# A new issue order, and a new split of copies and scalings between two engines, in a two-layer decoder trunk

## The chip, the cores and the metric

The kernel runs on one core of a Trainium2 chip. The core has a matrix engine (TensorE, PE), a vector engine (VectorE, DVE), a scalar engine (ScalarE, ACT), GpSimd (POOL) and SyncE (SP), each with its own instruction stream that it works off in order; transfers between device memory and the on-chip buffers are started by SP and ACT. The metric is the device time of one execution in microseconds (us), less is better.

## What is computed

The reference is a trunk of two layers over 256 tokens of width 1024, float32, conditioned by a vector `c`. Layer 0 has two groups of attention heads (a sliding window with sinks, and sparse attention with a compressed, a selected and a window branch); layer 1 has block attention, which for 256 tokens is causal attention with 16 heads.

```python
def reference(x, c, w_ada, b_ada, norm_g, w_in_even, ..., w_in_odd, w_out_odd, final_g):
    cos, sin = rope_tables(x.shape[1])
    c_act = jax.nn.silu(c)
    for layer in range(DEPTH):
        ada = jnp.einsum('bd,de->be', c_act, w_ada[layer]) + b_ada[layer]
        shift, scale, gate = jnp.split(ada, 3, axis=-1)
        h = rms_norm(x, norm_g[layer]) * (1.0 + scale[:, None, :]) + shift[:, None, :]
        if layer % 2 == 0:
            y = even_mixer(h, ...)      # oa*silu(za), ob*silu(zb), joined, @ w_out_even
        else:
            y = odd_mixer(h, ...)       # moba_attention(q, k, v) * silu(z), @ w_out_odd
        x = x + gate[:, None, :] * y
    return rms_norm(x, final_g)
```

## The kernel before

**Numbers.** Every large product is computed in three passes of a reduced format (`mm3`): a float32 operand is split into `hi` (a copy by ACT into `whi`, `hhi` or `ghi`) and `lo` (the difference, by DVE, into `wlo`, `hlo` or `glo`), and PE sums hi·hi, hi·lo and lo·hi in one bank. So each weight that is loaded (into one of five buffers `raw`, named raw_106 to raw_110 in the order listings) passes through ACT and DVE before PE can use it.

**Stages.** At the start, layer 0's shift and scale are made group by group (`START`, `start_ada`, `start_sums`) from parts of `w_ada`, which are loaded into whatever room is free: `qT`, `oT`, `gate`, `kTb`, `t`. Meanwhile rows of `w_in_even` come into `raw` (`start_row`: 1304 columns and 384 columns, two transfers each), and `start_mm` sums their products with the normalised input, 24 matmuls for each row block and 8 row blocks. `xs` holds the 256 tokens of `x`. Then come layer 0's two attention groups, its output projection, and beside them the sums over `w_ada` that layer 1 needs (DVE multiplies `raw` by `cz` and adds: the gate's sum into `acc`, the shift's and scale's into raw_110, whose last parts are loaded into raw_109). Then layer 0's result is added to `xs` (`t<-ps_pj,gate`, `xs<-xs,t`), the norm of layer 1 follows (`ISA` on `xs` is the sum of squares), then layer 1's projections, attention and output projection, and the last norm: for the last 256 columns of the last 128 tokens `xs<-ps_pj_101,xs`, the sum of squares, the root (ACT), the reciprocal (DVE), the multiplication by `final_g` (it lies in `bigA`), the scaling in three pieces, three transfers out.

**The order.** The body of the kernel issues nothing: class `Plan` records every operation with what it depends on (`record`), and `issue` (line 279) then emits all of them in the order of a table of 2985 numbers, `ORDER` (line 35), each engine getting its part of that one order. A second table, `FLIP` (line 164), holds numbers of operations that go to the other one of ACT and DVE than the code names: `copy`, `scaled` and `affine` ask for it in `either` (line 234). An engine waits at its next instruction until what it depends on is done, and nothing behind it passes. All instructions carry the line in `record` that makes the deferred call, L276 (in the changed kernel L275), so they are told apart by the names of their tiles.

```python
    def either(self, eng):
        other = self.vector if eng is self.scalar else self.scalar
        return other if len(self.ops) in FLIP else eng
```

Of the kernel before, what the change touches and what calls it, by code (L numbers as in the profile page):

```python
# [35 lines left out]
49 7 6 4 0 1 9 21 22 23 2 3 47 5 91 41 42 48 92 89 24 25 26 27 28 29 30 93 73 88 50 31 90 32 74 99 58 33 75 34  # L36
98 35 51 77 59 94 52 76 36 46 44 45 60 54 37 53 10 11 38 61 12 13 14 63 95 78 79 15 97 16 132 17 126 96 64 128
101 127 18 19 20 62 129 100 102 103 104 105 106 107 108 109 110 111 112 113 114 115 116 117 130 133 55 83 158
118 65 56 66 68 80 67 119 159 84 85 121 86 120 81 131 69 122 174 175 176 177 178 179 180 181 168 82 70 143 160
140 170 134 123 137 87 171 39 161 40 124 149 138 169 172 155 150 146 144 71 162 135 173 72 147 141 125 163 182  # L40
183 184 185 186 187 188 189 190 191 192 193 152 194 142 195 153 201 165 196 136 197 151 199 198 164 154 156 202
148 203 157 139 200 238 207 226 204 205 239 240 166 214 227 208 228 206 220 209 167 232 215 235 212 236 241 268
221 280 242 243 269 218 223 281 233 210 145 229 230 278 216 213 237 222 244 211 250 270 234 282 259 262 271 251
283 224 252 279 225 247 219 265 284 256 272 231 245 257 285 263 273 286 287 288 289 290 291 292 293 217 294 295
296 297 264 298 258 299 307 274 246 300 248 301 249 275 303 302 260 266 253 308 254 309 255 267 261 324 304 336
311 305 310 337 333 277 345 318 325 306 346 339 313 276 338 312 342 319 314 343 372 326 316 344 315 348 373 380
322 8 381 320 378 379 375 374 377 376 472 530 334 327 328 382 335 360 366 361 383 362 329 349 340 341 350 347
369 330 384 331 332 354 385 363 351 357 317 386 387 388 389 390 391 392 393 394 395 396 397 321 355 398 356 323
399 367 405 400 368 401 364 402 358 359 406 365 370 407 371 352 403 442 409 443 408 430 436 411 473 418 410 353
433 424 527 420 445 404 431 434 412 446 413 425 421 533 427 428 416 432 439 422 474 414 423 475 1003 939 476 691  # L50
477 417 415 435 444 466 429 451 440 441 447 437 463 478 480 482 484 479 481 483 485 486 487 438 488 460 419 489
495 454 455 491 490 469 470 493 464 492 426 496 448 499 457 467 494 497 471 529 456 500 509 501 449 498 510 511
524 450 502 503 617 525 452 458 618 465 619 620 531 453 468 461 550 506 462 942 459 556 512 551 513 813 514 526
507 554 504 557 508 552 505 521 555 522 534 518 536 553 515 537 516 541 538 519 606 542 520 938 539 517 535 607
528 544 543 608 937 547 540 676 564 565 566 567 568 569 576 694 577 612 578 579 609 580 581 588 589 590 613 558
523 610 611 591 592 593 549 600 601 602 559 639 545 692 603 604 621 614 622 623 624 560 695 561 625 548 562 563
570 571 615 572 605 573 626 627 640 631 628 629 632 641 574 575 630 582 693 583 633 634 635 814 935 636 643 644
645 646 584 642 638 585 940 586 587 647 594 595 670 596 597 669 546 598 637 599 668 648 649 816 650 651 663 653
661 662 696 697 698 699 700 671 654 701 652 702 664 703 818 943 689 819 936 655 817 656 43 657 665 658 704 666
705 706 667 707 708 815 709 660 710 711 659 672 673 712 713 674 714 715 716 944 717 941 746 747 748 749 945 532  # L60
683 675 946 947 948 949 754 950 951 952 953 750 752 954 955 956 957 756 753 958 959 960 961 677 684 1029 751 678
774 775 776 777 962 1032 682 757 758 780 679 680 963 685 681 718 820 782 781 964 778 719 821 686 759 784 687 720
755 822 721 722 786 688 723 965 823 971 824 779 724 966 972 785 868 869 870 871 760 967 787 968 872 761 878 969
783 768 973 974 975 976 977 978 979 980 876 981 982 983 984 763 874 985 986 987 988 769 762 788 880 1150 879 789
970 896 897 898 899 1030 1218 989 877 764 765 881 904 990 796 825 906 725 991 873 902 726 826 791 727 728 992
729 900 730 875 731 993 732 827 616 908 766 797 994 882 998 995 1000 1001 999 1031 767 1087 1088 1089 1090 996
790 905 770 1002 771 1648 1221 997 1033 772 828 1091 829 1004 830 690 831 1005 832 883 733 1093 1006 773 734
1097 1007 901 833 1095 834 792 1092 1008 793 794 891 1113 1114 1115 1116 1151 885 795 1009 1010 1011 1012 903
1034 798 799 1013 800 835 735 909 736 836 884 837 838 801 839 1152 1037 737 738 890 739 740 907 1014 886 887
1015 888 1121 1096 840 1350 741 1016 742 1094 841 1349 1123 842 1038 843 1017 1039 889 1040 844 1117 845 1035  # L70
743 910 846 1119 847 848 849 911 1219 892 850 1122 1041 1042 1043 851 1118 1153 1154 1155 1156 919 1018 1036 744
893 852 1098 853 894 1044 1045 1019 1046 913 1339 1047 854 1220 855 912 856 1048 1049 895 1050 1051 1052 1020
1053 1054 857 1157 1222 858 1419 859 1159 914 915 916 1418 1163 802 803 804 805 806 807 808 809 1160 1021 1161
917 1022 1099 1223 918 1124 1179 1180 1181 1182 1120 1100 1023 745 1164 920 921 922 1055 1056 1102 1024 1057
1189 1058 1059 1107 1060 1025 1226 1227 923 1228 1125 1183 1061 1062 1126 1108 860 810 1063 1064 1229 1230 1026
1101 1027 1187 1162 861 1340 862 863 1127 1065 1231 864 1133 1232 1233 1234 1028 865 1235 1185 1224 1236 1237
1103 1341 1104 1105 924 925 926 927 928 929 930 931 1106 1158 1225 1426 1128 811 1276 1277 1278 1279 866 1351
1423 1109 1134 1422 1110 1111 1066 1165 1188 1238 1282 1239 1240 1241 1067 1112 1284 1068 1166 1286 1069 1174
1070 1242 1352 1243 1129 1130 1184 1131 1244 1285 1071 1245 1072 1073 1167 1074 1280 1075 1427 1246 1247 1248
1249 1250 1251 1252 1253 1254 1132 1420 1186 1190 1076 1077 812 1255 1173 1135 1136 1137 1168 1191 1421 1302  # L80
1303 1304 1305 1138 1436 1342 1343 1344 1345 1312 1428 1169 1287 1306 1170 1171 1429 1192 1256 867 1078 1172
1079 1257 1258 1080 1199 1308 1259 1260 1313 1261 1262 1263 1264 1265 1281 1266 1267 1268 1283 1269 1081 1082
1310 1437 1083 1194 1175 932 1176 1177 1084 1450 1311 1270 1346 1451 1178 1288 1452 1424 1646 1193 1271 1272
1273 1085 1453 1195 1196 1274 1197 1289 1086 1353 1354 1355 1356 1198 1200 1425 1359 1139 1140 1141 1142 1143
1144 1145 1146 1147 1148 1307 933 1309 1275 1432 1440 1433 1201 1361 1202 1203 1357 1454 1430 1204 1444 1445
1290 1446 1291 1447 1448 1363 1442 1449 1292 1149 1293 1294 1431 1205 1206 1207 1208 1209 1210 1211 1212 1213
1214 1379 1380 1381 1382 1438 1297 1314 934 1508 1296 1295 1315 1439 1317 1316 1298 1362 1299 1215 1300 1493
1455 1364 1441 1456 1492 1457 1216 1462 1347 1463 1301 1458 1385 1464 1358 1459 1217 1318 1322 1465 1319 1360
1434 1320 1460 1461 1323 1468 1469 1365 1321 1387 1470 1366 1443 1466 1367 1324 1325 1368 1326 1471 1467 1327
1474 1435 1374 1496 1472 1369 1370 1526 1497 1371 1328 1329 1330 1331 1332 1333 1334 1335 1336 1337 1389 1509  # L90
1372 1383 1527 1373 1390 1384 1375 1494 1376 1377 1386 1534 1535 1388 1558 1536 1378 1391 1475 1392 1537 1495
1393 1538 1559 1394 1560 1528 1473 1395 1400 1396 1510 1397 1399 1561 1338 1562 1511 1398 1476 1529 1348 1563
1401 1402 1403 1477 1404 1478 1498 1479 1405 1406 1407 1408 1409 1410 1411 1412 1413 1414 1499 1530 1415 1539
1649 1540 1531 1416 1650 1588 1417 1512 1513 1541 1542 1564 1565 1480 1481 1543 1486 1487 1482 1488 1483 1489
1484 1490 1485 1491 1544 1500 1532 1545 1778 1566 1546 1504 1547 1548 1533 1549 1567 1550 1655 1568 1551 1501
1552 1717 1553 1554 1505 1502 1555 1556 1656 1557 1506 1503 1514 1515 1516 1517 1582 1651 1507 1653 1583 1569
1839 1518 1584 1652 1570 1571 1572 1573 1574 1575 1576 1589 1659 1519 1590 1520 57 1521 1591 1522 1657 1577 1523
1578 1524 1592 1593 1525 1654 1594 1595 1596 1579 1598 1580 1660 1581 1597 1605 1606 1585 1599 1601 1600 1667
# [1302 lines left out]
```

## Time and profile before

| | |
|---|---|
| Time, median of 3 runs | 294.72 us (294.68 to 314.98) |
| Profiled execution: time, span | 295.43 us, 293.7 us |
| PE, DVE, ACT busy | 283.5, 253.0, 201.2 us |
| Chain of work that ended last | PE 73%, DVE 13%, DMA 8%, issue 2%, ACT 2% |
| Moved by transfers | 71.76 MB, mean 244 GB/s |

The span is what the profiler saw from the first to the last instruction; 1.73 us of the profiled execution's time lie outside it. The busy time of PE counts each matmul up to a modelled end, so that matmuls that overlap fill the time between them. The chain is followed back from the last instruction, at each step to what released it.

### The profile page before, as it was taken

The page shows a single profiled execution, that of the slowest core. Times are in us where ns is not written, and L with a number is a line of the kernel's source. Part 1 is how long each engine was busy: PE and PEld are TensorE (multiplying, and loading weights), DVE is VectorE, ACT ScalarE, POOL GpSimd, SP SyncE. Part 2 cuts the span into 40 slices and gives each one's busy share as a digit, 9 for nine tenths or more (in the row PEclk, how much of TensorE's full clock was granted, in tenths as well). Part 3 has the DMA queues.
Part 4 walks back from the last instruction along what each step waited for, and adds up shares of the span by engine and source line. Part 5 has one row for each costly group of instructions (what it writes and reads, how often), then busy time and mean ns, then how long its engine had stood idle before and what let it go on. Part 6 is the DMA issues. An engine that isn't in the chain of part 4 may idle for free.

```text
span 293.7 us, 6077 instructions
## 1 busy us (share of the span) xinstructions
PE 283.5 (97%) x2244; PEld 243.5 (83%) x2244; DVE 253.0 (86%) x612; ACT 201.2 (69%) x513; POOL 5.5 (2%) x27
## 2 busy tenths in 40 slices
PE   8989999999999999999899999999999999999991
PEld 7868888997789888777667799999799899887891
DVE  0669999999999999999899868898699889889973
ACT  5554746695999999996398744466667377783821
POOL 2100000000000000000000000000000000000000
PEclk9999999999999999999999999999999999999998
DMA  7999999987996787799996449608927661604003
GB/s 260 364 385 377 383 355 353 311 287 237 342 400 212 264 281 293 213 323 361 305 372 216 146 143 329 243 4 296 351 71 249 237 234 34 227 27 145 1 15 129
DMA packets 50557, 71.76 MB, mean 244 GB/s; under 512 B 2792, under 2 KB 36192, under 8 KB 50528
## 3 DMA queue, kind: packets, MB, share of 16 engines
q1 hardware_dynamic: 50128, 70.95, 70.7%
q10 hardware_dynamic: 400, 0.43, 0.4%
q8 instruction: 17, 0.28, 0.4%
q14 instruction: 12, 0.10, 0.1%
HBM read 70.32 MB, written 1.06 MB: 243 GB/s over the span
## 4 chain that ended last, share of the span: by engine, by line
PE 73%; DVE 13%; DMA 8%; issue 2%; ACT 2%; SPq 0%; DVEq 0%
PE ps_pj L276 49%; PE ps_s L276 9%; PE ps_pt L276 6%; DVE raw L276 5%; PE ps_o L276 4%; PE ps_m L276 4%; DMA kTb<-in_w_ada_dram 3%; DMA raw<-in_w_ada_dram 2%; DVE wlo L276 2%; DMA qT<-in_w_ada_dram 2%; DMA xs<-in_x_dram 1%; DVE t L276 1%; DVE oT L276 1%; ACT t L276 1%; DVE bigA L276 1%
## 5 line engine op out<-in xcount | busy, mean ns | idle before, releaser
L276 ACT CAST whi<-raw 128x512 fp32r<-128x512 f32 (+2 forms) x108 | 71.6, 689 | 33.6 <-PE ps_pj L276 15.8
L276 DVE TENSOR_TENSOR wlo<-raw,whi 128x512 fp32r<-128x512 f32 (+2 forms) x92 | 70.8, 792 | 6.4 <-ACT whi L276 6.4
L276 PE MATMUL ps_pj<-hlo,whi 128*128 128x256 f32 x256 | 70.8, 284 | 0.0
L276 PE MATMUL ps_pj<-hhi,wlo 128*128 128x256 f32 x256 | 70.0, 284 | 0.3 <-DVE wlo L276 0.3
L276 PE MATMUL ps_pj<-hhi,whi 128*128 128x256 f32 x256 | 69.9, 284 | 0.0
L276 PEld LDWEIGHTS ps_pj<-hlo,whi 128*128 128x128 f32 x256 | 48.0, 189 | 0.6 <-issue 0.3
L276 PEld LDWEIGHTS ps_pj<-hhi,wlo 128*128 128x128 f32 x256 | 47.4, 189 | 0.7 <-DVE wlo L276 0.5
L276 PEld LDWEIGHTS ps_pj<-hhi,whi 128*128 128x128 f32 x256 | 47.4, 188 | 0.3
L276 ACT ACTIVATE sm<-sm,mn 128x256 f32<-128x256 f32 (+1 forms) x58 | 25.9, 449 | 6.9 <-DVE mn L276 6.9
L276 PE MATMUL ps_pj<-whi,hhi 128*128 128x512 f32 (+2 forms) x72 | 25.8, 368 | 0.5 <-ACT hhi L276 0.4
L276 PE MATMUL ps_pj<-whi,hlo 128*128 128x512 f32 (+2 forms) x72 | 26.1, 374 | 0.0
L276 PE MATMUL ps_pj<-wlo,hhi 128*128 128x512 f32 (+2 forms) x72 | 26.0, 370 | 0.0
L276 DVE SCALAR_TENSOR_TENSOR wlo<-raw,whi 128x512 fp32r<-128x512 f32 x32 | 20.6, 686 | 3.7 <-ACT whi L276 3.6
L276 PE MATMUL ps_pj<-wlo,ghi 128*128 128x512 f32 (+1 forms) x56 | 20.4, 368 | 0.0
L276 PE MATMUL ps_pj<-whi,ghi 128*128 128x512 f32 (+1 forms) x56 | 20.4, 369 | 0.0
L276 PE MATMUL ps_pj<-whi,glo 128*128 128x512 f32 (+1 forms) x56 | 20.0, 367 | 0.0
L276 ACT ACTIVATE sm<-sm,rc 128x256 f32<-128x256 f32 (+1 forms) x41 | 17.3, 449 | 2.3 <-DVE rc L276 2.3
L276 DVE SCALAR_TENSOR_TENSOR raw<-raw,cz,raw 128x1024 f32<-128x1024 f32 x14 | 17.9, 1276 | 1.0 <-DMA raw<-in_w_ada_dram 0.9
L276 DVE SCALAR_TENSOR_TENSOR acc<-raw,cz,acc 128x1024 f32<-128x1024 f32 x14 | 17.9, 1278 | 0.1
L276 PEld LDWEIGHTS ps_pj<-whi,hhi 128*128 128x128 f32 x72 | 13.6, 188 | 2.7 <-ACT hhi L276 1.2
L276 PEld LDWEIGHTS ps_pj<-whi,hlo 128*128 128x128 f32 x72 | 13.5, 188 | 2.5 <-DVE hlo L276 0.8
L276 PE MATMUL ps_pt<-ident,sm 128*128 128x128 f32 x87 | 15.5, 279 | 0.0
(252 smaller groups left out, 599.7 us busy)
## 6 DMA issues: line engine op xcount, KB each, us to landing
raw<-in_w_in_odd_dram SPq DMA_DIRECT2D x16, 1024.0 KB, 7.5
raw<-in_w_ada_dram SPq DMA_DIRECT2D x8, 1024.0 KB, 6.2
raw<-in_w_ada_dram SPq DMA_DIRECT2D x16, 512.0 KB, 5.2
raw<-in_w_in_even_dram SPq DMA_DIRECT2D x8, 652.0 KB, 7.2
raw<-in_w_in_even_dram SPq DMA_DIRECT2D x5, 1024.0 KB, 7.7
raw<-in_w_out_even_dram SPq DMA_DIRECT2D x4, 1024.0 KB, 5.4
raw<-in_w_out_odd_dram SPq DMA_DIRECT2D x4, 1024.0 KB, 5.0
qT<-in_w_ada_dram SPq DMA_DIRECT2D x12, 256.0 KB, 6.2
```

The source lines that it names most:

```text
L276: self.ops.append(dict(key=eng.key, deps=deps, fn=lambda: getattr(real, name)(*args, **kw)))
```

## The change

Only the two tables differ. `ORDER` holds the same 2985 numbers in another order from the first row to the last, `FLIP` has 78 entries instead of 74 (24 new ones, 20 of the old ones gone). A line of each:

```diff
 ORDER = [int(i) for i in """
-49 7 6 4 0 1 9 21 22 23 2 3 47 5 91 41 42 48 92 89 24 25 26 27 28 29 30 93 73 88 50 31 90 32 74 99 58 33 75 34
+93 159 7 0 1 9 21 22 23 24 25 26 27 28 29 30 2 6 5 50 31 32 33 34 35 36 51 52 54 55 56 42 41 47 46 37 10 11 3 58
...
 FLIP = {int(i) for i in """
-67 124 194 210 298 314 414 763 768 790 791 796 884 885 890 912 913 918 1101 1102 1107 1127 1128 1133 1167 1168
+61 62 67 76 82 124 194 199 314 398 403 414 488 493 762 768 790 791 796 884 885 890 891 912 913 918 919 1101 1102
...
```

PE has the same 1884 operations, SP the same 127 transfers. Of the operations that ask for either engine, DVE has 614 recorded instructions and ACT 433 in both kernels, but others: at the start one copy into `bigA` (128x512), two affine operations `oT<-bigA,shs` (128x256) and one half of a scaling of `xs` go from DVE to ACT and one small copy `asb<-ps_m` to DVE; in layer 0's attention DVE has five scalings `sm<-sm,rc` of 128x256 and none of 128x128 up to the last load into raw_109, where it had one of 128x128 and none of 128x256, and ACT one copy `pT<-ps_pt` more. The listings below show three places; a row's "x2" means two instructions of that kind in a row.

**The start.** SP's first transfers, before:

```order
L276 DMA xs<-in_x_dram 128x1024 x2
L276 DMA qT_104<-in_w_ada_dram 128x4x128
L276 DMA raw_106<-in_w_in_even_dram 128x1304
L276 DMA qT_103<-in_w_ada_dram 128x4x128
L276 DMA raw_106<-in_w_in_even_dram 128x384
L276 DMA qT_103<-in_w_ada_dram 128x4x128
L276 DMA qT_104<-in_w_ada_dram 128x4x128
L276 DMA oT<-in_w_ada_dram 128x2x256 x2
L276 DMA qT_105<-in_w_ada_dram 128x2x256 x2
L276 DMA gate<-in_w_ada_dram 128x2x256 x2
L276 DMA kTb<-in_w_ada_dram 128x2x256 x2
L276 DMA raw_107<-in_w_in_even_dram 128x1304
```

and now:

```order
L275 DMA raw_106<-in_w_in_even_dram 128x384
L275 DMA raw_107<-in_w_in_even_dram 128x384
L275 DMA xs<-in_x_dram 128x1024 x2
L275 DMA qT_103<-in_w_ada_dram 128x4x128 x2
L275 DMA qT_104<-in_w_ada_dram 128x4x128 x2
L275 DMA raw_106<-in_w_in_even_dram 128x1304
L275 DMA qT_105<-in_w_ada_dram 128x2x256 x2
L275 DMA oT<-in_w_ada_dram 128x2x256 x2
L275 DMA gate<-in_w_ada_dram 128x2x256 x2
L275 DMA kTb<-in_w_ada_dram 128x2x256 x2
L275 DMA raw_107<-in_w_in_even_dram 128x1304
```

The two 384-column pieces of `raw` (of row blocks 0 and 1) now stand first, ahead of `xs`; the four transfers into `qT_103` and `qT_104` are together; the 1304-column piece of row block 0 and `oT` stand later; ahead of the end of `kTb` there is one transfer more, raw_107's 384 columns. PE's matmuls up to the eight that read `kTb`, before:

```order
L276 MATMUL ps_o_70<-whi_113,hhi 128x408
L276 MATMUL ps_pj_99<-wlo_117,hhi 128x408
L276 MATMUL ps_pt_90<-whi_113,hhi 128x256
L276 MATMUL ps_o_70<-wlo_117,hhi 128x408
L276 MATMUL ps_pj_100<-whi_112,hhi 128x512
L276 MATMUL ps_pt_90<-wlo_117,hhi 128x256
L276 MATMUL ps_s_98<-ident,t_94 128x128
L276 MATMUL ps_pj_101<-wlo_116,hhi 128x512
L276 MATMUL ps_pj_100<-wlo_116,hhi 128x512
L276 MATMUL ps_s_97<-wlo_116,hhi 128x512
L276 MATMUL ps_m_68<-kTb,cz 32x128 x8
```

and now:

```order
L275 MATMUL ps_m_68<-oT,cz 32x128 x8
L275 MATMUL ps_o_70<-ones 128x128
L275 MATMUL ps_pj_101<-whi_112,hhi 128x512
L275 MATMUL ps_pj_101<-wlo_116,hhi 128x512
L275 MATMUL ps_pt_90<-whi_113,hhi 128x256
L275 MATMUL ps_s_98<-whi_112,hhi 128x512
L275 MATMUL ps_pt_90<-wlo_117,hhi 128x256
L275 MATMUL ps_m_68<-kTb,cz 32x128 x8
```

(`whi`, `wlo` are the split weights, `hhi` the split input; `ones` are products that nobody reads.) Counted from the first such product of the kernel, 13 matmuls of row block 0 stood ahead of `kTb`, and 9 stand there now; the other four stand behind it.

**DVE in the attention of layer 0**, around the two sums that free raw_109 for its last load (raw_110 is the running sum, `ISA` the masked scores and their row minimum, `rc` the reciprocals), before:

```order
L276 TENSOR_TENSOR wlo_117<-raw_106,whi_113 128x1024
L276 SCALAR_TENSOR_TENSOR raw_110<-raw_108,cz,raw_110 128x1024
L276 ISA sm_126,mn_137<-ps_s_98,tb 128x256
L276 ISA mn_137 128x1
L276 ISA bigA,mn_137<-ps_s_97,tb 128x128
L276 ISA mn_137 128x1
L276 TENSOR_TENSOR wlo_118<-raw_107,whi_114 128x1024
L276 SCALAR_TENSOR_TENSOR raw_110<-raw_109,cz,raw_110 128x1024
L276 RECIPROCAL rc_143<-den_140 128x4
L276 TENSOR_TENSOR rc_143<-rc_143,gt 128x4
L276 SCALAR_TENSOR_TENSOR raw_110<-raw_109,cz,raw_110 128x1024
L276 TENSOR_SCALAR sm_126<-sm_126,rc_143 128x256
```

and now:

```order
L275 ISA sm_126,mn_137<-ps_s_98,tb 128x256
L275 ISA mn_137 128x1
L275 TENSOR_TENSOR wlo_116<-raw_106,whi_112 128x1024
L275 TENSOR_TENSOR wlo_117<-raw_106,whi_113 128x1024
L275 SCALAR_TENSOR_TENSOR raw_110<-raw_108,cz,raw_110 128x1024
L275 RECIPROCAL rc_143<-den_140 128x4
L275 TENSOR_TENSOR glo<-oT,ghi 128x512
L275 TENSOR_TENSOR rc_143<-rc_143,gt 128x4
L275 TENSOR_TENSOR asb_85<-ps_m_68,asb_86 128x256
L275 TENSOR_TENSOR wlo_118<-raw_107,whi_114 128x1024
L275 SCALAR_TENSOR_TENSOR raw_110<-raw_109,cz,raw_110 128x1024 x2
```

The two sums that read raw_109 now follow each other directly; the reciprocal and its product with `gt` that stood between them stand ahead, as does the addition into `asb_85`.

**DVE's last instructions**, before:

```order
L276 TENSOR_TENSOR xs<-xs,t_95 128x256
L276 TENSOR_TENSOR xs<-ps_pj_101,xs 128x256
L276 ISA t_93,parts<-xs,parts 128x256
L276 ISA parts 128x1
L276 TENSOR_TENSOR xs<-xs,bigA 128x256
L276 RECIPROCAL parts<-parts 128x1
L276 TENSOR_TENSOR xs<-xs,bigA 128x256
L276 TENSOR_SCALAR t_94<-xs,parts 128x320 x2
```

and now:

```order
L275 TENSOR_TENSOR xs<-xs,t_95 128x256
L275 TENSOR_TENSOR xs<-xs,bigA 128x256
L275 TENSOR_TENSOR xs<-ps_pj_101,xs 128x256
L275 ISA t_93,parts<-xs,parts 128x256
L275 ISA parts 128x1
L275 TENSOR_TENSOR xs<-xs,bigA 128x256
L275 RECIPROCAL parts<-parts 128x1
L275 TENSOR_SCALAR t_94<-xs,parts 128x320 x2
```

One of the two multiplications of `xs` by `bigA` that stood behind the last `xs<-ps_pj_101,xs` now stands ahead of it.

## Rows read from the trace of the kernel before

**Rows 1.** The page's first part: busy time, share of the span and instructions of each engine.
```profile
PE 283.5 (97%) x2244; PEld 243.5 (83%) x2244; DVE 253.0 (86%) x612; ACT 201.2 (69%) x513; POOL 5.5 (2%) x27
```

**Rows 2.** Table of stretches: start:end and length, busy us (instructions) by engine, clock, DMA share, GB/s.
```profile
0.00:20.00 20.00, 17.64 (x172) 15.56 (x173) 7.91 (x20) 10.15 (x19) 3.17 (x18) 1.00 0.95 333
20.00:57.00 37.00, 37.00 (x250) 31.61 (x249) 34.58 (x74) 22.18 (x53) 0.00 (x0) 1.00 1.07 367
57.00:80.00 23.00, 23.00 (x228) 19.64 (x227) 22.53 (x79) 18.89 (x61) 0.38 (x3) 1.00 0.86 281
80.00:103.00 23.00, 23.00 (x212) 19.75 (x212) 22.86 (x79) 22.81 (x73) 0.00 (x0) 1.00 0.81 285
103.00:125.00 22.00, 22.00 (x187) 17.46 (x184) 22.00 (x54) 21.89 (x63) 0.32 (x1) 1.00 0.78 266
125.00:135.00 10.00, 10.00 (x64) 7.71 (x62) 9.96 (x24) 9.71 (x28) 0.00 (x0) 1.00 0.95 336
...
146.00:166.00 20.00, 18.86 (x90) 13.20 (x90) 18.01 (x43) 17.22 (x42) 0.61 (x2) 1.00 0.82 280
166.00:288.00 122.00, 121.38 (x996) 110.75 (x996) 103.21 (x229) 72.85 (x172) 1.00 (x3) 1.00 0.48 161
```

**Rows 3.** Timeline of PE, 16.5 to 19 us: start, us busy, what, [idle before <- releaser].
```profile
17.10 0.40 PE L276 MATMUL ps_s<-wlo,hhi 128*128 128x512 f32 x1
18.61 0.64 PE L276 MATMUL ps_m<-kTb,cz 128*32 128x128 f32 x16 [1.12 <-DMA kTb<-in_w_ada_dram]
```

**Rows 4.** Chain of waits, 0 to 24 us: start, length, what.
```profile
5.06 5.94 DMA qT<-in_w_ada_dram
...
11.01 7.55 DMA kTb<-in_w_ada_dram
...
20.72 0.18 PE ps_o L276
...
21.79 1.39 PE ps_s L276 x6
```

**Rows 5.** DMA queues, 16 to 19 us: packets, MB, share of 16 engines' time.
```profile
q8 instruction: 1, 0.02, 2.4%
```

**Rows 6.** The page's third part, the same over the whole span.
```profile
q8 instruction: 17, 0.28, 0.4%
```

**Rows 7.** Groups by shape, the scalings of the softmax on DVE: us busy, mean ns.
```profile
L276 DVE TENSOR_SCALAR sm<-sm,rc 128x256 f32<-128x256 f32 x8 | 2.8, 347 | 0.0
...
L276 DVE TENSOR_SCALAR sm<-sm,rc 128x128 f32<-128x128 f32 x9 | 2.4, 279 | 0.1
...
L276 DVE COPY pT<-ps_pt 128x384 f32<-128x384 f32 x2 | 1.1, 550 | 0.0
```

**Rows 8.** The same on ACT: the exponentials ahead of those scalings.
```profile
L276 ACT ACTIVATE sm<-sm,mn 128x256 f32<-128x256 f32 x29 | 14.6, 505 | 6.9 <-DVE mn L276 6.9
```

**Rows 9.** Chain of waits, 128 to 156 us.
```profile
132.77 1.20 DVE raw L276
...
134.45 6.87 DMA raw<-in_w_ada_dram
...
145.22 1.14 DVE wlo L276
...
153.64 0.50 PE ps_pj L276
```

**Rows 10.** Waits of PE, 140 to 154 us: us in total, times, longest.
```profile
PE ps_s L276 <- DVE wlo L276: 0.8, 1, 0.8
```

**Rows 11.** Timeline of DVE, 286.8 to 294 us.
```profile
287.47 0.42 DVE L276 TENSOR_TENSOR xs<-ps_pj,xs 128x256 f32<-128x256 f32 x1 [0.90 <-PE ps_pj L276]
...
288.57 0.43 DVE L276 TENSOR_TENSOR xs<-xs,bigA 128x256 f32<-128x256 f32 x1
...
288.99 0.41 DVE L276 TENSOR_TENSOR xs<-xs,bigA 128x256 f32<-128x256 f32 x1
```

**Rows 12.** Timeline of ACT, 286.5 to 287.1 us.
```profile
286.66 0.42 ACT L276 ACTIVATE t<-xs 128x256 f32<-128x256 f32 x1 [1.42 <-DVE xs L276]
```

255 rows, old and new, of tables (FLIP, ORDER) are left out of this document.

## Prediction

> **What bounds the kernel now.** I read the busy times first, then a table of stretches, the chain of waits, and the timelines at the few places where the matrix engine stops. PE is busy for 283.5 of 293.7 us [rows 1], and between 20 and 57 us and from 166 to 288 us it has next to no gap: 37.00 of 37.00 and 121.38 of 122.00 us [rows 2]. [...] The reader should see that a new order cannot shorten PE's work, since PE has the same 1884 operations before and after. It can only change the stops, and these are few: 2.36 us of the first 20 us, 1.14 us of 146 to 166 us, 0.62 us of 166 to 288 us [rows 2], and the end, where PE has nothing left. (Ends of matmuls are modelled, so true stops are somewhat longer; the differences below are taken between starts.) A gain of 2%, 5.9 us, would need more than all the stops ahead of the last matmul that the table shows together. About 2% is also what a measurement of this kernel can tell from no change.
>
> PE is not alone, though. From 57 to 135 us, in layer 0's attention, DVE is busy for 22.53 + 22.86 + 22.00 + 9.96 = 77.35 of 78 us, so it has 0.65 us to spare, and ACT is as full from 80 to 125 us (22.81 and 21.89 of 45 us) [rows 2]. In the chain, DVE's sums end at 133.97, that frees the buffer for the last load of layer 1's weights, the load takes 6.87 us, and through sums, norm and split the first matmul of layer 1 comes at 153.64 [rows 9]. From there on PE has no room to catch up. So three places decide: the start, DVE's load of work up to 134 us, and the end.
>
> **The start.** SP now sends one transfer more ahead of the end of kTb: 128 x 384 x 4 bytes, 0.20 MB. At the 367 GB/s of the stretch behind [rows 2] that is 0.54 us. In the kernel before, PE starts its last matmul ahead of kTb at 17.10 and goes on at 18.61, when kTb has landed [rows 3, 4]. With kTb 0.54 us later it goes on at 19.15. It also has nine instead of 13 matmuls of row block 0 ahead of that wait, so four (two of 408 and two of 512 columns) are still owed behind it: 2 x 0.18 + 2 x 1.39/6 = 0.82 us [rows 4]. Together that is +1.36 us if PE streams from there, as it does before, and this is the upper bound. The lower bound comes from the other thing that hits kTb. One instruction fetch falls between 16 and 19 us; it took 2.4% of 16 engines' 3 us, which is 1.15 us on one of them [rows 5]. If that fetch comes behind kTb now, kTb lands at 18.56 + 0.54 - 1.15 = 17.95, PE goes on at about 18.0, 0.61 us earlier than before, and with 0.82 us owed the term is +0.2. I take +0.6: nearer to the middle, because DVE has a copy, two affine operations and half a scaling less to do there, and ACT, at 22.18 of 37 us [rows 2], has room for them. The input xs, which now stands behind 0.39 MB (1.1 us), I cost at nothing: the chain at the start runs through parts of w_ada (qT, 5.06 to 11.00 us) [rows 4], and the last of those stands behind less than before; uncovered it would cost the same 1.1 us.
>
> [...] No row before shows where the fetch will fall, so I keep the value between.
>
> **DVE up to the last load.** Up to the second sum that frees raw_109, DVE has five scalings of 128x256 where it had one of 128x128, and one copy of 128x384 less: 5 x 0.347 - 0.279 - 0.550 = +0.91 us [rows 7]. Of that, 0.65 us is the slack counted above. If all the slack can be used, +0.26 is left; if none, +0.91. I take +0.5, nearer to the first, since the copies moved at the start relieve DVE as well. Everything behind (the load of 6.87 us, the norm) moves with it. ACT gives up these scalings where it was full; that is worth nothing on this path, because in 103 to 125 us DVE does not wait at all (22.00 of 22.00) [rows 2].
>
> **The change of layers.** The subtraction wlo that PE waits for at 146.41 now stands ahead of the second t<-ps_pj, so that PE's wait of 0.8 us [rows 9, 10] shortens by one such step, 0.64 us (half of 1.28). But the first matmul of layer 1 hangs on the norm, and ahead of the sum of squares DVE still has the same instructions: two wlo, three t and three xs in another order. What PE gains at 146 us it waits at 153: 0, with -0.64 as the lower bound. In layer 1 the same work stands on the same engines but for a few affine operations; I take 0, and as bounds the stops of 146 to 166 us either way, -1.1 and +1.1.
>
> **The end.** One multiplication by bigA, 0.41 us, stood between the reciprocal and the last scalings [rows 11]. It now stands ahead of the last xs<-ps_pj, where DVE waits 0.90 us for PE. It overwrites what ACT squares from 286.66 to 287.08 [rows 12], so it runs from about 287.1 to 287.5 and pushes the last addition, at 287.47, by some 0.05 us. Term: -0.35, with bounds -0.41 and 0.
>
> **The sum** is +0.6 + 0.5 + 0 + 0 - 0.35 = +0.75 us on the profiled execution's 295.43 us, so 296.2 us. The median of the runs is 0.71 us below that execution, so I forecast 295.5 us: no change that can be told.
>
> **Rivals.** First, a gain: the fetch falls behind kTb (+0.2), the slack of DVE takes all but 0.26, the shorter wait at 146 us stays won (-0.64), layer 1 loses half of its stops (-0.6), the end gives 0.35. That is -1.1 us, 293.6 us, and with all of layer 1's stops and nothing lost at the start or on DVE 292.6 us. For it speaks that each stop has a near cause; against it that DVE and PE are both full where the work was added.
>
> Second, slower: the five moved scalings need a reciprocal of sums that ACT's exponentials leave, and DVE works in order. Before, ACT waited there; now DVE would. One exponential takes 0.505 us [rows 8]; if DVE waits for one at each of the five places, that is +2.5 us, the slack being spent already, and the time is 295.5 + 2.5 = 298.0 us. It decides when DVE's stops between 57 and 135 us exceed some 1.5 us. Against it: the new order puts other DVE work between reciprocal and scaling. To pass 2%, 300.6 us, each of the 29 exponentials of that shape would have to stop DVE for 0.18 us.
>
> Third, nothing moves: later work at the start is taken up by stops up to 57 us, and the time stays within 0.3 us of 294.7. This lies inside the forecast's own range.
>
> **Chances.** The forecast, with the third, 0.5 (its own range 294.4 to 297.0 us); the gain 0.32; slower by waits of DVE 0.18. The range that leaves out no more than 2 in 10 goes from 292.6, the gain's far end, to 298.2, just past the second rival. Faster by over 2% would need every stop gone: 0.03. Slower by over 2% is the far part of the second rival: 0.05. Within 2%: 0.92.
>
> **What would show it.** In the changed kernel's timeline of PE the matmuls on kTb should start at about 19.1 (at 18.0 in the gain) and the q8 row of that stretch says where the fetch fell. DVE's busy time between 57 and 135 us should be full, with its stops under 1 us; the last load into raw_109 should be issued at 134.5 to 135.5, the first matmul of layer 1 should start near 154.7, and from the last matmul to the end it should be 0.35 us shorter. I am wrong if that first matmul starts ahead of 153 or behind 157 us, or if PE loses more than 2 us in layer 1.

## The result, and the profile after

The changed kernel takes 298.06 us (median of six executions) against 294.72 us: a ratio of 1.011, with a 95% interval of 1.008 to 1.014. One of the six took 317.12 us at a mean granted clock of 0.85 and is left out of the ratio; the other five, at 0.99 to 1.00, took 296.88 to 298.43 us (median 297.99). The kernel is slower by 1.1%, within the 2% of "no change that can be told". That is inside the predicted range, 0.1 us from its end, outside the forecast's own range (294.4 to 297.0 us), and 2.6 us above the 295.5 us forecast. Its profiled execution took 298.13 us with a span of 296.1 us, 2.4 us more than before.

The busy times of the changed kernel [rows 1]:

```profile
PE 286.2 (97%) x2244; PEld 246.2 (83%) x2244; DVE 251.3 (85%) x612; ACT 200.9 (68%) x513; POOL 6.6 (2%) x27
```

PE's busy time has grown by 2.7 us although it has the same operations. The table of stretches says where; the columns are those of [rows 2].

```profile
0.00:20.00 20.00, 17.52 (x137) 15.07 (x137) 5.98 (x17) 11.14 (x22) 2.88 (x16) 0.93 0.91 305
20.00:57.00 37.00, 37.00 (x266) 31.28 (x266) 31.77 (x71) 19.91 (x41) 0.32 (x1) 0.99 1.06 369
57.00:80.00 23.00, 23.00 (x202) 20.26 (x202) 22.43 (x66) 18.99 (x58) 0.29 (x4) 1.00 0.75 240
80.00:103.00 23.00, 23.00 (x224) 19.03 (x223) 22.55 (x96) 22.46 (x78) 0.00 (x0) 1.00 0.83 291
103.00:125.00 22.00, 22.00 (x199) 18.21 (x197) 21.93 (x55) 21.52 (x66) 0.00 (x0) 1.00 0.72 246
125.00:135.00 10.00, 10.00 (x70) 7.43 (x69) 10.00 (x23) 10.00 (x26) 0.06 (x1) 1.00 0.96 348
...
146.00:166.00 20.00, 18.57 (x92) 13.75 (x92) 18.17 (x38) 15.49 (x37) 1.19 (x2) 1.00 0.94 312
166.00:288.00 122.00, 122.00 (x996) 110.83 (x995) 104.68 (x235) 73.71 (x174) 1.22 (x2) 1.00 0.49 163
```

Three things differ from before. The clock of the first stretch is 0.93 and no longer 1.00; PE's matmuls of the first 20 us are 137 where they were 172; and from 166 us on PE has no stop left at all (122.00 of 122.00, before 121.38). DVE and ACT are nearly as full in layer 0 as they were: from 57 to 135 us DVE is busy for 76.91 of 78 us (before 77.35).

To place the loss I took six starts from the timelines of PE and SP. "End of the start" is the 191st of the start's 192 products over `w_in_even`: the same amount of that work in both kernels, though not the same product. In the kernel before the 192nd stands among the products of the next stage, in the changed kernel it follows at once. The two products, before and after:

```profile
56.98 0.39 PE L276 MATMUL ps_pj<-whi,hlo 128*128 128x512 f32 x1
...
59.10 0.40 PE L276 MATMUL ps_s<-whi,hlo 128*128 128x512 f32 x1
```

```profile
60.59 0.40 PE L275 MATMUL ps_pj<-wlo,hhi 128*128 128x512 f32 x1
60.82 0.40 PE L275 MATMUL ps_pj<-whi,hlo 128*128 128x512 f32 x1
```

| us | before | after | difference |
|---|---|---|---|
| first of those 192 products | 14.20 | 16.16 | +1.96 |
| PE goes on with `kTb` | 18.61 | 21.34 | +2.73 |
| end of the start | 56.98 | 60.59 | +3.61 |
| from there to the last load into raw_109 | 77.47 | 78.33 | +0.86 |
| from there to the first matmul of layer 1 | 19.19 | 19.19 | 0.00 |
| from there to PE's last matmul | 133.52 | 131.77 | -1.75 |
| from there to the end of the span | 6.5 | 6.2 | -0.3 |

The four lower rows and the +3.61 add up to +2.42 us, the difference of the spans. So between these two executions the change loses 3.6 us in the first 60 us and 0.9 us up to the last load, and wins some 2 us back in layer 1 and at the end. The table compares one execution of each; the experiments say what of it the times of many executions show.

The timeline of PE in the start of the changed kernel, with the row that answers to [rows 3] last:

```profile
14.51 0.35 PE L275 MATMUL ps_m<-blk,asb 128*128 128x2 f32 x2 [0.83 <-ACT asb L275]
...
15.38 0.33 PE L275 MATMUL ps_s<-ident,t 128*128 128x128 f32 x1 [0.18 <-DVE t L275]
...
16.16 0.50 PE L275 MATMUL ps_s<-whi,hhi 128*128 128x512 f32 x1 [0.35 <-ACT hhi L275]
...
21.34 0.64 PE L275 MATMUL ps_m<-kTb,cz 128*32 128x128 f32 x16
```

PE stops for 0.83, 0.18 and 0.35 us ahead of its first product, the `kTb` matmuls come 2.73 us later than before, and ahead of them no DMA is named any more. The chain of waits of the same stretch [rows 4]:

```profile
6.30 7.26 DMA raw<-in_w_in_even_dram
13.59 0.62 ACT whi L275
...
15.62 0.50 ACT hhi L275
16.16 0.50 PE ps_s L275
```

The chain no longer runs through `qT` and `kTb`. It runs through raw_106's 1304 columns, which SP issues at 6.30 us and which land at 13.56, through the copy `whi` and the scaling `hhi` on ACT, to the first product.

### The profile page after: what moved, and what is told of

The parts are those of the page before. It is cut to its first block, busy times and chain, and to the rows that moved or that the text cites. A ratio compares the mean times of both kernels' runs of the same rounds, so it can differ in the third digit from the quotient of the medians.

```text
span 296.1 us, 6088 instructions
## 1 busy us (share of the span) xinstructions
PE 286.2 (97%) x2244; PEld 246.2 (83%) x2244; DVE 251.3 (85%) x612; ACT 200.9 (68%) x513; POOL 6.6 (2%) x27
## 4 chain that ended last, share of the span: by engine, by line
PE 73%; DVE 14%; DMA 5%; issue 3%; ACT 2%; SPq 2%; ACTq 0%; DVEq 0%
PE ps_pj L275 49%; PE ps_s L275 9%; PE ps_pt L275 7%; PE ps_o L275 5%; DVE raw L275 5%; PE ps_m L275 4%; DVE wlo L275 3%; DMA raw<-in_w_in_even_dram 2%; DMA raw<-in_w_ada_dram 2%; SPq L275 2%; DVE t L275 2%; DVE xs L275 1%; DVE oT L275 1%; ACT t L275 1%; DVE sm L275 1%
## 5 line engine op out<-in xcount | busy, mean ns | idle before, releaser
L275 PE MATMUL ps_pj<-whi,hhi 128*128 128x512 f32 (+2 forms) x72 | 26.5, 378 | 0.8 <-ACT hhi L275 0.8
L275 ACT ACTIVATE sm<-sm,rc 128x128 f32<-128x128 f32 (+1 forms) x36 | 15.5, 444 | 0.3 <-DVE rc L275 0.3
L275 ACT ACTIVATE whi<-raw 128x512 fp32r<-128x512 f32 x16 | 9.7, 626 | 8.7 <-PE ps_pj L275 8.7
```

The lines of the kernel that those rows point to most:

```text
L275: self.ops.append(dict(key=eng.key, deps=deps, fn=lambda: getattr(real, name)(*args, **kw)))
```

## The experiments

All times are medians. The ratio to the kernel before (runs on the same chip) has its 95% interval behind it. No kernel here leaves out work.

**Is it the start at all?** The changed kernel, with the start (all that feeds the 192 products) in the order and on the engines of before. Layer 0's first transfers stay behind the start's last one, so that they can't get in its way.

```diff
-DMA raw_106<-in_w_in_even_dram 128x384
-DMA raw_107<-in_w_in_even_dram 128x384
 DMA xs<-in_x_dram 128x1024 x2
+DMA qT_104<-in_w_ada_dram 128x4x128
+DMA raw_106<-in_w_in_even_dram 128x1304
...
```

> The changed kernel with the start of before, as in e2b_start_old, but with the transfers of layer 0 (sinks, tables, first weights) held behind the last transfer of the start on SP: in e2b_start_old two of them went out between, and ACT waited 2.5 us for the last row block at 52.7 us. Theory A, the rest of the change gains 0.8 us at the change of layers and 0.3 us at the end and costs nothing in layer 0: time 292.8 to 294.0 us, under that of before (294.5). Rival B, DVE's larger load in layer 0 costs 0.5 us or more: 294.3 us or more.

Measured: 294.72 us, 1.0015 [1.0003, 1.0026], the time of rival B. The start of before gives back 3.3 us (2.8 us by the ratios): practically the whole loss, and 0.4 us against the kernel before are left. From the end of the start to the last load into raw_109 this kernel takes 78.8 us, 0.4 more than the changed one; the hold is not shown to be the reason, since the third join below, which holds nothing back, takes 78.9. So the start costs 2.8 to 3.3 us, and the rest of the change, by this run and the next, next to nothing (+0.4 and +0.3 us by the ratios).

The profile of this kernel also says how far a single one can be trusted at `kTb`. Up to there its engines have the order of before, operation for operation, and PE goes on with `kTb` without a stop:

```profile
17.20 0.40 PE L269 MATMUL ps_s<-wlo,hhi 128*128 128x512 f32 x1
17.53 0.65 PE L269 MATMUL ps_m<-kTb,cz 128*32 128x128 f32 x16
```

In the three other kernels below that have this start unchanged it is 17.59, 17.61 and 17.96 us, again without a stop. The stop of [rows 3] and the 18.61 us are those of one execution in five.

**The other half of that.** The kernel before up to the change of layers, the changed order from there to the end.

```diff
 TENSOR_TENSOR xs<-xs,t_95 128x256
+TENSOR_TENSOR xs<-xs,bigA 128x256
 TENSOR_TENSOR xs<-ps_pj_101,xs 128x256
...
```

> The kernel before up to the change of layers; from there on (output projection of layer 0, norm, layer 1, end) the changed kernel's order and engines. Theory: PE's lead at the end of layer 1 is 0.8 us, the end another 0.3 us shorter, time 293.2 to 293.9 us; with e2c_start_old the difference of the two is what layer 0 costs. Rival, the gain there in the changed kernel was only a late start being caught up: 294.2 us or more.

Measured: 294.51 us, 1.0011 [0.9996, 1.0027]: no gain that can be told, as the rival had it. In its trace layer 1 is as short as in the changed kernel (131.84 us from its first matmul to the last), but that first matmul comes 20.15 us after the last load into raw_109 where it came 19.19 before. The 1.75 us of the table are real in the sense that every kernel with the new order there shows them (131.76 to 132.04, against 133.36 to 133.52 with the old one), but here the first matmul comes later by more than half as much, and the time shows no gain.

**Three joins that say nothing.** The same question, with the table cut at a place. The first puts the new start ahead of the old remainder, the second the old start ahead of the new remainder, the third is the kernel with the old start without holding layer 0's transfers back.

```diff
-49 7 6 4 0 1 9 21 22 23 2 3 47 5 91 41 42 48 92 89 24
+93 159 7 0 1 9 21 22 23 24 25 26 27 28 29 30 2 6 5 50
...
```

> The kernel before, with the operations of the start (all up to the last product of row block 7) in the changed kernel's order and on its engines, the rest as before. Theory A, the whole loss is made at the start: PE ends the start 3.6 us late, as in the changed kernel (60.8 against 57.2 us), nothing in layer 0 gives it back, and the time is 297.3 to 298.5 us. Rival B, layer 0's old order has room for a late start and the loss comes from DVE's larger load there: 294.7 to 296.0 us.

```diff
-93 159 7 0 1 9 21 22 23 24 25 26 27 28 29 30 2 6 5 50
+49 7 6 4 0 1 9 21 22 23 2 3 47 5 91 41 42 48 92 89 24
...
```

> The changed kernel with the operations of the start in the order and on the engines of before. Theory A: the start ends near 57.2 us again and the time is 3.6 us below the changed kernel's, 293.3 to 294.7 us, so that what is left of the change gains up to 1 us. Rival B, the loss is in layer 0: 296.5 us or more.

```diff
 DMA kTb<-in_w_ada_dram 128x4x128
+DMA snk<-in_a_sinks_dram 128x8
+DMA tb<-in_tbl_b_dram 128x1056
...
 DMA raw_108<-in_w_in_even_dram 128x1304
```

> The changed kernel with the start's operations in the order and on the engines of before; the two orders are joined by the times at which the operations ran in the two traces, so that each engine works off the start exactly as before and the rest exactly as the changed kernel does. Theory A, the whole loss is made at the start (PE 3.5 us late at 57 us and again at 144 us): time 293.0 to 294.6 us. Rival B, part of the loss comes from DVE's larger load in layer 0: 295.5 us or more.

The three took 306.24 us (1.039 [1.037, 1.041]), 309.95 us (1.052 [1.048, 1.055]) and 297.38 us (1.011 [1.008, 1.014]). The seam of each makes a wait of its own. The waits of PE (first kernel), of SP (second) and of ACT (third) around the seam: us in total, times, longest.

```profile
PE ps_s L270 <- ACT whi L270: 3.5, 1, 3.5
```

```profile
SPq L269 <- DVE wlo L269: 24.4, 3, 20.1
```

```profile
ACT whi L269 <- DMA raw<-in_w_in_even_dram: 2.9, 2, 2.5
```

Their times say nothing about the change, and I draw on none of them. The starts themselves behaved as in the kernels that they came from: with the new start (first join) the first product came at 16.24 us and `kTb` at 21.41, with the old one (second and third) at 14.62 and 14.37 and at 17.96 and 17.59.

**The small pieces ahead of `xs`.** In the kernel before, only the two 384-column pieces are moved to the front of SP's transfers, as the change has them.

```diff
+DMA raw_106<-in_w_in_even_dram 128x384
+DMA raw_107<-in_w_in_even_dram 128x384
 DMA xs<-in_x_dram 128x1024 x2
...
-DMA raw_106<-in_w_in_even_dram 128x384
...
-DMA raw_107<-in_w_in_even_dram 128x384
```

> The kernel before with one thing changed: the two 384-column pieces (raw_106, raw_107) go out first, ahead of xs, as in the changed kernel; PE's order is that of before. Theory K, small pieces in front cost more than their bytes (the changed kernel had moved less by 8 us): kTb lands 1.0 to 1.6 us later and the time is 295.5 to 296.5 us. Rival K0, only the 0.20 MB count: kTb 0.5 us later, 295.0 to 295.4 us. Rival: it is hidden, 294.7 us.

Measured: 296.65 us, 1.0079 [1.0052, 1.0106]: +2.3 us by the ratio, from two transfers alone. In its trace the first product comes at 16.89 us and `kTb` at 20.11. And its counterpart, which moves the same bytes but not to the front: raw_107's 384 columns right behind `xs`.

```diff
 DMA xs<-in_x_dram 128x1024 x2
+DMA raw_107<-in_w_in_even_dram 128x384
...
-DMA raw_107<-in_w_in_even_dram 128x384
```

> The kernel before with raw_107's 384 columns (0.20 MB) moved on SP from behind kTb to right behind xs: the same bytes ahead of kTb as in the changed kernel, but xs still first. Theory K0 for the bytes alone: kTb 0.5 us later, 295.0 to 295.4 us. If the place behind xs also thins out the stream at 3 to 5 us, as it was with the small pieces first (0.35 MB less by 8 us), kTb is 1.4 us or more later and the time 295.8 us or more.

Measured: 294.74 us, 1.0014 [1.0000, 1.0027]: +0.4 us, although in its profiled execution PE stops for 1.76 us and goes on with `kTb` only at 19.50. So the 0.20 MB ahead of `kTb` cost about what I had put on them (0.54 us), and the place of the two pieces costs the rest, 1.9 us. The table of stretches from 3 to 5 us, in the same columns (the last is GB/s), of the kernel before, the changed one, the one with both pieces in front, and the one with a piece behind `xs`:

```profile
3.00:5.00 2.00, 2.00 (x12) 2.00 (x12) 0.00 (x0) 0.85 (x2) 0.00 (x0) 1.00 1.03 409
```

```profile
3.00:5.00 2.00, 2.00 (x11) 2.00 (x11) 0.00 (x0) 0.55 (x1) 0.00 (x0) 1.00 0.70 174
```

```profile
3.00:5.00 2.00, 2.00 (x11) 2.00 (x11) 0.00 (x0) 0.49 (x1) 0.00 (x0) 1.00 0.89 199
```

```profile
3.00:5.00 2.00, 2.00 (x11) 2.00 (x11) 0.00 (x0) 0.78 (x2) 0.00 (x0) 1.00 1.01 404
```

With the small pieces in front the stream carries 174 and 199 GB/s in these 2 us, otherwise 409 and 404. Part of that is only a shift, since the pieces themselves moved in the microsecond ahead. From 2 to 8 us, in the kernel before and in the one with both pieces in front:

```profile
2.00:8.00 6.00, 5.88 (x38) 5.48 (x37) 0.66 (x3) 4.25 (x7) 1.54 (x7) 1.00 0.93 347
```

```profile
2.00:8.00 6.00, 5.68 (x33) 5.35 (x32) 0.00 (x0) 2.14 (x2) 0.00 (x0) 1.00 0.95 293
```

That is 0.32 MB less in 6 us (0.38 MB in the changed kernel, at 284 GB/s), some 0.8 to 0.9 us of transfer at the 404 GB/s above. `xs` shows it first. ACT's squares of `xs` (tile view: ns min/median/max, first and last start), before and after:

```profile
L276 ACT ACTIVATE t<-xs x2: 1056/1056/1057, 4.6 to 5.9; 128x1024 f32<-128x1024 f32 x2
```

```profile
L275 ACT ACTIVATE t<-xs x2: 1052/1054/1056, 7.6 to 8.9; 128x1024 f32<-128x1024 f32 x2
```

They start 3.0 us later (2.5 in the kernel before with the pieces in front), where bytes alone (0.39 MB) would have made it 1.1. Why the stream is slow behind the small pieces I don't know. No run here took the pieces' row length and their place apart.

**Taking it back.** The changed kernel with `xs` first, raw_106's piece behind it, and raw_107's piece and its copy on ACT back behind raw_107's 1304 columns.

```diff
+DMA xs<-in_x_dram 128x1024 x2
 DMA raw_106<-in_w_in_even_dram 128x384
-DMA raw_107<-in_w_in_even_dram 128x384
-DMA xs<-in_x_dram 128x1024 x2
...
 DMA raw_107<-in_w_in_even_dram 128x1304
+DMA raw_107<-in_w_in_even_dram 128x384
```

> The changed kernel with xs first again, the 384 columns of row block 0 behind it, those of row block 1 (and the copy on ACT that reads them) behind its 1304 columns, as before. Theory K: kTb lands near 18.6 us again, PE's matmuls on it start 1.0 to 2.0 us earlier than in the changed kernel (21.34 us), time 296.0 to 297.2 us. Rival, raw_106's late 1304 columns and the lower clock behind them set PE's start: 297.5 us or more.

Measured: 295.67 us, 1.0043 [1.0030, 1.0057]: 2.4 us less than the changed kernel (2.0 by the ratios). Its table row of 3 to 5 us and its timelines of PE and ACT:

```profile
3.00:5.00 2.00, 2.00 (x11) 2.00 (x11) 0.00 (x0) 0.54 (x1) 0.00 (x0) 1.00 1.01 379
```

```profile
14.53 0.50 PE L270 MATMUL ps_s<-whi,hhi 128*128 128x512 f32 x1 [0.54 <-ACT hhi L270]
...
18.16 0.64 PE L270 MATMUL ps_m<-kTb,cz 128*32 128x128 f32 x16
```

```profile
6.39 0.18 ACT L270 ACTIVATE tiny<-ps_pt 128x8 f32<-128x8 f32 x1 [2.85 <-PE ps_pt L270]
6.46 1.05 ACT L270 ACTIVATE t<-xs 128x1024 f32<-128x1024 f32 x1
```

The stream is at 379 GB/s again, the first product starts at 14.53 us and `kTb` is served at 18.16: both within 0.5 us of where they were before the change. raw_106's large piece is there for ACT at 11.40 us (13.59 in the changed kernel), though its place behind the `qT` transfers is unchanged. ACT's order in the changed kernel has another instruction ahead of the squares of `xs`, which here waits for PE until 6.39 us. So a late `xs` holds ACT up only beyond that time: in the changed kernel for 1.0 of the 3.0 us.

**raw_106's 1304 columns**, which stand behind four `qT` transfers in the change: put ahead of them in the changed kernel, and, the other way round, put behind them in the kernel before.

```diff
 DMA xs<-in_x_dram 128x1024 x2
+DMA raw_106<-in_w_in_even_dram 128x1304
 DMA qT_103<-in_w_ada_dram 128x4x128 x2
 DMA qT_104<-in_w_ada_dram 128x4x128 x2
-DMA raw_106<-in_w_in_even_dram 128x1304
```

> The changed kernel with one transfer moved: raw_106's 1304 columns go out behind xs and ahead of the four into qT, as early as before. Theory A1, this transfer's late landing (13.56 against 8.21 us) holds up ACT's and DVE's queues and with them the first product: the first product starts at 14.0 to 14.8 us instead of 16.16, PE's granted clock stays at 1.00 in 16 to 22 us, and the time is 295.0 to 296.3 us. Rival A2, the start is late because of kTb and the four matmuls owed behind it, as predicted: kTb is as late as in the changed kernel, time 297.3 us or more.

```diff
 DMA qT_104<-in_w_ada_dram 128x4x128
-DMA raw_106<-in_w_in_even_dram 128x1304
 DMA qT_103<-in_w_ada_dram 128x4x128
...
+DMA raw_106<-in_w_in_even_dram 128x1304
 DMA oT<-in_w_ada_dram 128x2x256 x2
```

> The kernel before with the same transfer moved the other way: raw_106's 1304 columns go out behind the four into qT. Theory A1: landing near 12 us, the first product 1.0 to 2.0 us late, time 296.0 to 297.5 us. Rival A2: nothing but the place of kTb matters, and that stays, time within 0.4 us of 294.7.

Measured: 297.32 us, 1.0095 [1.0072, 1.0118], so 0.7 us less than the changed kernel, a difference that the two intervals don't separate; and 294.81 us, 1.0015 [1.0001, 1.0029], so +0.4 us on the kernel before. Both times are those of rival A2. In the second the first product comes 1.4 us later (15.60 us) and PE goes on with `kTb` at 18.83 without a stop. That is 0.2 us later than in the profile of before, as if the stop of [rows 3] took the delay up, but 1.2 later than in the executions without that stop; by the end of the start 0.3 to 0.8 us are left (57.28 against 56.48 to 56.98). The chain of the changed kernel runs through this transfer, and yet it is not the main cause; with it early again, the first product came only 0.3 us sooner (15.86 us); `xs` was late there too, with ACT's first square at 7.0 us.

**The four matmuls owed behind `kTb`**, alone in the kernel before:

```diff
-MATMUL ps_o_70<-whi_113,hhi 128x408
...
-MATMUL ps_pj_100<-wlo_116,hhi 128x512
...
 MATMUL ps_m_68<-kTb,cz 32x128 x8
...
+MATMUL ps_o_70<-whi_113,hhi 128x408
+MATMUL ps_o_70<-wlo_117,hhi 128x408
+MATMUL ps_pj_100<-whi_112,hhi 128x512
+MATMUL ps_pj_100<-wlo_116,hhi 128x512
```

> The kernel before with four matmuls of row block 0 (two of 408, two of 512 columns) moved from ahead of kTb's matmuls to behind them, nothing else. Theory: PE waits for kTb that much longer and owes them behind it, +0.82 us, 295.2 to 295.8 us. Rival, later stops take it up: within 0.3 us of 294.6.

Measured: 295.06 us, 1.0016 [1.0002, 1.0031]: +0.5 us. The timeline of PE:

```profile
18.32 0.65 PE L270 MATMUL ps_m<-kTb,cz 128*32 128x128 f32 x16 [1.26 <-DMA kTb<-in_w_ada_dram]
```

PE waits here for the same `kTb`, and from that row to the end of the start it takes 39.20 us where it took 38.37: the 0.82 us of the prediction to 0.01. The median shows +0.5, and its interval (0.1 to 0.9 us) holds 0.82 too.

**The clock.** In the changed kernel PE's clock falls; the table of stretches around `kTb` (the clock stands third from the end):

```profile
16.00:18.00 2.00, 1.83 (x8) 1.55 (x9) 1.87 (x4) 2.00 (x6) 0.00 (x0) 0.78 1.12 390
18.00:20.50 2.50, 2.50 (x22) 1.81 (x22) 1.73 (x3) 0.94 (x2) 0.00 (x0) 0.50 1.03 384
20.50:22.00 1.50, 1.50 (x29) 1.09 (x27) 0.02 (x1) 0.25 (x1) 0.00 (x0) 0.99 1.10 386
```

From 18 to 20.5 us the granted clock is 0.50. Ahead of that, from 13.5 to 16 us, PE was busy for 1.30 of 2.50 us:

```profile
13.50:16.00 2.50, 1.30 (x8) 0.72 (x6) 1.77 (x5) 2.17 (x5) 0.00 (x0) 1.00 1.02 340
```

The same start in the first join does the same (1.12 of 2.50 us busy, then 0.54). Not every such stretch is followed by a lower clock: in the kernel with one piece behind `xs` PE was busy for 1.00 of the 2.50 us from 18 to 20.5 us, and the clock was 1.00 there and up to 22 us. The transfer into `kTb` landed at 20.14 us, but the nine matmuls ahead of it were not done, and PE came to it 1.2 us later. To price this, the changed kernel got 12 more products of `ones`, which nobody reads, in those stops; what counts is the clock from 18 to 20.5 us, where it was 0.50, and when PE comes to `kTb`:

```diff
+MATMUL ps_o_70<-ones 128x128 x6
 MATMUL ps_m_68<-blk,asb_85 128x2
-MATMUL ps_o_70<-ones 128x128
+MATMUL ps_o_70<-ones 128x128 x4
...
+MATMUL ps_o_70<-ones 128x128 x3
 MATMUL ps_s_97<-whi_112,hhi 128x512
```

> The changed kernel with 12 more of the products of ones (128x128, nobody reads them) in PE's stops between 13.7 and 16.2 us, ahead of the first product of row block 0. [...] Theory C, part of the loss is the clock: clock 1.00 there, kTb's matmuls at 20.3 us, time 296.8 to 297.4 us. Rival, the clock does not count because kTb's landing sets the end of that stretch: 297.8 us or more.

Measured: 297.36 us, 1.0096 [1.0078, 1.0114]. In its table the clock from 18 to 20.5 us is 1.00:

```profile
18.00:20.50 2.50, 2.50 (x40) 1.84 (x33) 1.69 (x4) 0.62 (x2) 0.00 (x0) 1.00 1.05 382
```

PE goes on with `kTb` at 19.47 us instead of 21.34. The median is 0.7 us lower (0.4 by the ratios), which the intervals again don't separate, and this profile is of the fastest of its six executions (295.68 us). The mean granted clock of whole executions fits: in the changed kernel's five it is 0.990 and 0.988 in the two that took 298.13 and 298.43 us, and 0.995 to 0.998 in the three that took 296.88 to 297.99; with the added products it is 0.995 to 0.998 in all six. So the fall seems to come in some executions only, at about 1 us each; that this difference is the clock's alone is not shown. In the kernels with the large transfer early, or with the small pieces behind `xs`, the clock stayed at 1.00 in these stretches of the profiled execution, with the same nine matmuls.

## Why the prediction was right and wrong

The time fell into the stated range by 0.1 us, and the far end of that range came from a rival (waits of DVE for exponentials) that did not happen. That part is luck.

**The start, +0.6: this is the step that failed.** It was +2.8 to +3.3 us by time. I counted the bytes that now stand ahead of `kTb`, and took the stream's rate from the stretch behind (367 GB/s) as if it held from the first transfer on. The runs put four pieces in place of that one: the small pieces in front of `xs`, +2.3 us in the kernel before; the bytes alone, +0.4 (not to be added to the first); the late 1304 columns, +0.4; the four owed matmuls, +0.5. The first, third and fourth make 3.2 us, near what undoing the whole start gives back. That they add up is not shown, and the three small ones stand hardly clear of the noise; the changed kernel with the small pieces back, at +1.3 us, fits the sum. Two of them stand in the prediction and were priced about right (0.54 and 0.82 us). Two were missed. That `xs` stands behind 0.39 MB I named, put at 1.1 us uncovered, and costed at nothing, because the chain at the start ran through `qT`; it became 3.0 us, and the chain moved to what needs `xs` and raw_106. That raw_106's large piece now stands behind four transfers I showed in the listing and did not price at all. The base of the step was weak as well: I took the wait for `kTb` at 18.61 us for a property of the order, and four other executions of this start have no such stop (17.53 to 17.96 us).

The lower bound of that step (+0.2) hung on the instruction fetch falling behind `kTb`. The row that answers to [rows 5], for 16 to 18 us of the changed kernel:

```profile
q8 instruction: 1, 0.02, 3.1%
```

The fetch lies ahead of the landing at 20.14 us, so the case of that bound did not come. The changed kernel has 17 fetches of 0.28 MB in all, as before [rows 6]; what decides when one comes, no run here shows. That a fetch ahead of `kTb` puts its landing off by the fetch's whole time (1.15 us on one engine) was an estimate of mine, which no run shows either. With the step at its upper bound, +1.36 us, the sum gives 296.2 us, nearer to the measured time than my value, though that accounts for 0.7 us of the miss only.

**DVE up to the last load, +0.5 (bounds +0.26 and +0.91): right in kind, near the upper bound.** The table has +0.86. The other kernels bear it out: from the end of the start to that load the kernels with the old order take 77.4 to 77.5 us (five traces), those with the new order and the new start 78.3 to 78.5 (four). So the added work shows as if next to none of DVE's slack could be used; its idle time from 57 to 135 us even grew, from 0.65 to 1.09 us. The rival of waits on exponentials did not come. The waits of DVE from 57 to 139 us:

```profile
DVE t L275 <- ACT vz L275: 0.5, 1, 0.5
DVE sm L275 <- PE ps_s L275: 0.2, 1, 0.2
DVE bigA L275 <- PE ps_s L275: 0.2, 1, 0.2
```

They sum to 0.9 us (before 0.3), none of them is for an exponential, and 1.5 us was the point from which that rival would decide. It gave the right size, 298.0 us, for the wrong reason.

**The change of layers and layer 1, 0 (bounds -0.64 to 0, and 1.1 either way): right for the change of layers, missed in layer 1.** The chain of waits around them [rows 9]:

```profile
138.92 6.20 DMA raw<-in_w_ada_dram
...
158.11 1.90 PE ps_pj L275 x7
```

The load takes 6.20 us (before 6.87), is issued 4.47 us later, and the first matmul of layer 1 comes 4.47 us later, as the prediction had it: nothing won there. The waits of PE [rows 10]:

```profile
PE ps_pj L275 <- ACT hhi L275: 0.8, 1, 0.8
PE ps_s L275 <- DVE wlo L275: 0.6, 1, 0.6
```

The wait for `wlo` is 0.6 instead of 0.8 us (I had it shorter by 0.64), and PE waits 0.8 us for `hhi` ahead of layer 1's first product, where it waited 0.4. Behind it PE gains 1.75 us, against the -1.1 that I had as the bound, where PE has no stop left. By the two orders only two transpositions of 128x128 have moved ahead of that first matmul, so nearly all of it is stops that are gone, more of them than the modelled ends of the matmuls let the table show. Two other executions of the order of before took 18.5 us for the step that takes 19.19 in the table, so single rows of this part are good to some 0.7 us. Without the new start, the new order from here on is worth nothing that can be told (294.51 us).

**The end, -0.35: right.** The timeline of DVE's tail [rows 11]:

```profile
289.81 0.43 DVE L275 TENSOR_TENSOR xs<-xs,bigA 128x256 f32<-128x256 f32 x1 [0.64 <-ACT t L275]
290.19 0.42 DVE L275 TENSOR_TENSOR xs<-ps_pj,xs 128x256 f32<-128x256 f32 x1
...
291.28 0.42 DVE L275 TENSOR_TENSOR xs<-xs,bigA 128x256 f32<-128x256 f32 x1
```

One multiplication runs at 289.81, ahead of the last `xs<-ps_pj`, and only one is left behind the sum of squares. From the last matmul to the end it is 0.3 us shorter.

**The sum** missed by its first term: 2.2 to 2.7 us too small, which is the 2.6 us between 295.5 and 298.06. In the traces the four terms are +3.6, +0.9, -1.75 and -0.3 us, so there a gain in layer 1 that I had at 0 hides part of the start's miss. The profile of before was taken in an execution at 295.43 us, some 1 us above the 294.4 us that this kernel takes in the median of all its runs. That is why the traces show +2.4 us where the ratio shows +3.3.

## What to carry to other kernels

Price a transfer that is moved to the front of a kernel by what it does to the ones behind it, not by its bytes (behind the two pieces ACT's first square of `xs` came 2.5 and 3.0 us later, where their bytes made 1.1): look where the input lands that the first computation needs, and follow every transfer that the listing moves, not only those on the chain of before. When the chain of waits of the old kernel runs through one load, the new order may make another load the last one; ask for each input of the first product when it will be there. A wait that a profile shows may belong to that execution only; look for it in a second one before a term is built on it. If parts of a large reordering are to be tested apart, keep the transfers of the later part behind those of the earlier one, or the seam makes a wait larger than the effect (3.5 and 20.1 us in two joins here, against 2.8 to 3.3).

## What was not expected of the hardware

Two transfers of 384 columns (rows of 1.5 KB) at the front of the queue left the stretch from 3 to 5 us at 174 to 199 GB/s, against 379 to 409 in the three rows without both of them in front, and the one from 2 to 8 us at 284 and 293 against 347 in the kernel before; the cause is open. The granted clock fell to 0.50 for 2.5 us behind a stretch in which PE was busy for 1.30 of 2.50 us; with products of `ones` in the stops it was 1.00. It was 1.00 as well behind a stretch with 1.00 of 2.50 us busy in another kernel, so what makes it fall is not shown. Five executions of one start put the matmuls on `kTb` at 17.53 to 18.61 us, and only the latest of them with a stop.
